# Moving the weight buffers and one activation tile in SBUF, in a decoder trunk of two layers

## The chip, the cores and the metric

One core of one Trainium2 chip runs the whole kernel. The metric is device time in microseconds, the median of the runs shown.

## The reference

Two layers act on 256 tokens of 2048 channels in float32. Layer 0 mixes tokens with an S5 state-space model and a gated projection, layer 1 with a causal depthwise convolution of 31 taps between two projections; each is followed by a SwiGLU network of 5632 hidden channels. Every sub-layer ends in a residual and a LayerNorm, with scale, shift and gate from a condition vector c. What matters here are the dense products and the loop around them, cut to its core:

```
for i in range(DEPTH):                       # DEPTH = 2
    mod = silu(c) @ ada_w[i] + ada_b[i]      # six vectors of 2048
    h = x * (1 + sc_m) + sh_m
    y = s5_mixer(h, ...)   if i == 0 else conv_mixer(h, ...)
    x = layer_norm(ALPHA * x + (1 + gt_m) * y)
    h = x * (1 + sc_f) + sh_f
    g, v = split(h @ w_gu)                   # 2048 x 11264
    y = (silu(g) * v) @ w_down               # 5632 x 2048
    x = layer_norm(ALPHA * x + (1 + gt_f) * y)
```

The result is wanted in float32 accuracy, and the kernel gets it from three products of split operands.

## The kernel before

Channels lie on partitions, tokens along the free dimension. X holds the residual stream; h (32 KB in each partition) holds the input of the current product as two parts, hh and hl, a value rounded to float32r and the rest; f2 (24 chunks of 128 hidden channels, 48 KB) holds the same of the hidden layer.

**Weights.** Every product reads its weights once from memory, in units of 512 rows by 512 columns. Unit (L834 ff.) takes a raw buffer filled by a DMA of the SP queue, ACT rounds it into whi (L835), DVE writes the rest into wlo (L836). The pool w has two buffers of each, 8 KB a partition, so that one unit is converted while the other is used.

**Matmuls.** gemm walks over the units. For each chunk of 128 input channels it computes hi times hi, wlo times hi and whi times lo. In the wide form (L891) a 128x128 block of tokens and channels of x, out of h or f, is held in TensorE and 512 columns of whi or wlo stream past it; each unit gives 24 such matmuls, each with a held block of its own. In the narrow form (L895), used where the output must come out with channels on partitions, a 128x128 block of the weights is held and 256 columns of h or f stream. A panel after each LayerNorm (L1007, Entry.panel) is like the narrow form, but streams 258 columns out of a tile raw, which is h itself or the space of f2, in rows of 258. Results of the wide form are turned back by L907. Loading the next held block overlaps the current matmul.

**Beside the matmuls.** DVE adds up the condition's projections (L703) from rawa, and computes the taps of some convolution channels (L1633); the other channels go through TensorE (L1672, four matmuls side by side, each with 32 held columns).

**Where the tiles lie.** Pools are placed one behind the other in each partition: the long-lived tiles (X, h and others), four raw buffers, further constants, the pool w, the pools s and ada of small tiles, and then f2, or the convolution's tiles (V, pad, vs, lw) in the same space. f0 and f1 are the pools of f2 for the two layers. Addresses in bytes in a partition, as the programs before and after have them:

| tile | before | after | modulo 512, before / after |
|---|---|---|---|
| h | 37824 | 37824 | 448 / 448 |
| whi, first and second | 113344, 121536 | 113344, 121600 | 192, 192 / 192, 256 |
| wlo, first and second | 129728, 137920 | 129856, 138112 | 192, 192 / 320, 384 |
| first tile of the pool s | 146112 | 146304 | 192 / 384 |
| f2 of layer 0 | 177088 | 177280 | 448 / 128 |
| f2 of layer 1 | 177088 | 177568 | 448 / 416 |

A held block of h or f starts a multiple of 512 bytes, and a moving row of whi or wlo a multiple of 2048 bytes, behind its tile's start; so the last column tells all starts modulo 512. "Distance" below is the start of the moving operand minus that of the held block loaded beside it.

Of the kernel before, what the change touches and what calls it, by code (L numbers as in the profile page):

```python
# [11 lines left out]
F32 = mybir.dt.float32  # L12
F32R = mybir.dt.float32r
# [6 lines left out]
P = 128  # L20
# [487 lines left out]
def kernel(  # L508
# [71 lines left out]
    def load_unit(src, k0, kn, segs, eng=nc.sync):  # L580

        r = raws[0].tile([P, 4, 512], F32, tag="raw", name="raw")
        if kn > 4:
            r = r.rearrange("p a b -> p (a b)").rearrange("p (k n) -> p k n", k=kn)
        raws.append(raws.pop(0))
        at = 0
        for c0, n in segs:
            eng.dma_start(r[:, :kn, at:at + n], src[k0 * P:(k0 + kn) * P, c0:c0 + n].rearrange("(k p) n -> p k n", p=P))
            at += n
        return r  # L590

    class Later:


        def __init__(self):
            self.now, self.todo = 0, []
# [17 lines left out]
    def queue_behind(instructions):  # L614

        st = ExitStack()
        for i in instructions:
            st.enter_context(tc.issue_after(i.ins))
        return st
# [206 lines left out]

    class Unit:


        def __init__(self, wp, wsrc, k0, kn, segs, behind=()):  # L830
            r = load_unit(wsrc, k0, kn, segs)
            self.hi = wp.tile([P, 4, 512], F32R, tag="whi", name="whi")
            self.lo = wp.tile([P, 4, 512], F32R, tag="wlo", name="wlo")
            with queue_behind([*behind, *held_back]):  # L834
                m1 = nc.scalar.copy(out=self.hi[:, :kn], in_=r[:, :kn])  # L835
                m2 = nc.vector.tensor_tensor(out=self.lo[:, :kn], in0=r[:, :kn], in1=self.hi[:, :kn].bitcast(F32), op=SUB)  # L836
            self.marks = [m1, m2]
            nonlocal newest
            newest = self
# [219 lines left out]
    def residual(y, gt, ch, stats=None):  # L1059

        for k in range(2):
            nc.vector.scalar_tensor_tensor(
                out=X[:, ch + k], in0=y[:, k], scalar=gt[:, ch + k:ch + k + 1], in1=X[:, ch + k], op0=MUL, op1=ADD)
        if stats is None:
            return
        i, z = ch // 2, X[:, ch:ch + 2]
        if i == 0:
            later.put(1, lambda: stats.begin(z))
            later.put(1, lambda: stats.add(0, z))
            for p in range(1, 8):  # L1070
                later.put(1 if p == 1 else 2 + p % 2, lambda p=p: stats.move(X[:, 2 * p:2 * p + 2]))
        elif i == 1 and later.todo:
            later.put(1, lambda: stats.add(1, z))
        else:
            stats.add(i, z)
# [23 lines left out]
    def add_later(ys, gt, ch, stats, sp):  # L1099

        yt = [sp.tile([P, 2, SEQ], F32, tag="sg", name="yt", bufs=2).rearrange("p a b -> p (a b)") for _ in range(2)]
        nc.scalar.copy(out=yt[0], in_=ys[0].rearrange("p a b -> p (a b)"))
        nc.vector.tensor_copy(out=yt[1], in_=ys[1].rearrange("p a b -> p (a b)"))
        for i in range(2):
            turning.put(2, lambda i=i: turned(yt, 256 * i, lambda b: residual(b, gt, ch + 2 * i, stats)))

    def gu_cols(f):
        return [(f * P, 256), (DFF + f * P, 256)]
# [205 lines left out]
    w = s5.work  # L1314
# [71 lines left out]
    mctx = ExitStack()  # L1386

    def start_dense():
        nonlocal const2, wp
        const2 = ctx.enter_context(tc.tile_pool(name="const2", bufs=1, reuse_waits="tile"))  # L1390
        wp = mctx.enter_context(tc.tile_pool(name="w", bufs=2, reuse_waits="tile"))
        ready.append(Unit(wp, s5_w_glu[0], 0, 4, [(0, 256), (D, 256)]))

    const2 = wp = ln_col = wtap = fold32 = row_of = None
# [14 lines left out]
    with tc.manual_schedule(engines={mybir.EngineType.PE}):  # L1409
# [9 lines left out]
        for ct in range(NCH - 1):  # L1419
            now, y = coming, None  # L1420
            if (ct + 1) % 4 == 1 and ct < 12:
                load_x(ct // 4 + 1)
            s5.weights_in(ct + 1)
            n = plan[ct + 1]
            ada_units(n > 0)
            with queue_behind([] if ct else [s5.made]):
                tabs[ct + 1] = s5.tables(ct + 1, [last])
            if held:
                y = s5.read_out(*held)
            u, uh, last = inputs(ct + 1)  # L1430
            ada_units(n > 1)
            coming = ct + 1, u, s5.drive(ct + 1, uh)
            if not ct:
                s5.weights_out(0, d_col[:, 0:1], last)
            s5.weights_out(ct + 1, d_col[:, ct + 1:ct + 2], last)
            ada_units(n - 2)
            if ct == NCH - 2:
                raws[:] = [rawp]
                more.close()
                s5.keep_ctx.close()  # L1440
                start_dense()
            scan(ct, now, y)
            if ct % 4 == 3 and ct < 11:
                extra = quarter_steps(ct // 4 + 2)
            with queue_behind([s5.last]):
                next(extra, None)
# [53 lines left out]
    def entry_raw(fp):  # L1500
        t = fp.tile([P, 24, 2, SEQ], F32R, tag="f2", name="raw").rearrange("p a h b -> p (a h b)")
        return t[:, 0:2 * NCH * EW]
# [5 lines left out]
    with mctx:  # L1508
# [4 lines left out]
        def enter(name, stats, i, k, raw, pairs):  # L1513

            layer, j = (i, 3) if k == 0 else (i + 1, 0)
            ada.finish(layer, j)
            ada.finish(layer, j + 1)
            g, b = ln_gb(i, k)
            hg, hb = fold(name, g, b, mod[layer][:, j + 1], mod[layer][:, j])
            e = Entry(sp, stats, raw, hg, hb, scaled(name + "xg", g, ALPHA), scaled(name + "xb", b, ALPHA))  # L1520
            for p in range(pairs):
                later.put(1 + p // 2, lambda p=p: e.split(p))
            return e
# [4 lines left out]
        for i in range(8):  # L1528
            if i == 7:
                fp = f0ctx.enter_context(tc.tile_pool(name="f0", bufs=1, reuse_waits="tile"))  # L1530
# [204 lines left out]
        for q in range(4):  # L1735
            if q == 3:
                ada.hold = True
                raw = entry_raw(fp)
                entry = enter("f1", stats, 1, 0, raw, 6)
            wide = q in (1, 2)  # L1740
            ys = gemm(cv_w_pw2[0], 0, NCH, [(512 * q, 512)], xh, wp, feed if q == 0 else None,
                      ahead=(ffn_w_gu[1], gu_cols(0)) if q == 3 else None, wide=wide)
            if wide:
                add_later(ys, mod[1][:, 2], 4 * q, stats, sp)
            for i in range(0 if wide else 2):
                residual(ys[i], mod[1][:, 2], 4 * q + 2 * i, stats)
                if q == 3:
                    entry.split(6 + i)
            if q == 0:
                cvctx.close()  # L1750
                fp = f1ctx.enter_context(tc.tile_pool(name="f1", bufs=1, reuse_waits="tile"))
        ada.hold = False
        stats = Stats("ln11", sp, True)
        ada.rate = 0.5
# [26 lines left out]
```

## Time and profile before

| | |
|---|---|
| median of 3 runs | 2292.09 us (2291.61 to 2294.86) |
| profiled execution, as timed | 2298.0 us |
| its span, first to last instruction | 2295.8 us |
| mean granted TensorE clock | 0.992 |
| busy: PE, PEld, DVE, ACT, POOL | 2223.8, 1799.3, 1691.1, 1015.6, 156.0 us |
| read from HBM | 573.72 MB, 251 GB/s over the span |

PE is TensorE's matmuls, PEld its weight loads. The duration of a matmul in the profile reaches to its modelled end and overlaps the next one; what a stream of them costs is the spacing of their starts. The chain of work is followed back from the last instruction through what released each step.

### The profile page before, as it was taken

To read this page: it belongs to the slowest core of one execution; us is meant where nothing else is said; L and a number is where in the kernel's file an instruction comes from. 1 tells how busy PE (TensorE), PEld (TensorE's weight loads), DVE (VectorE), ACT (ScalarE), POOL (GpSimd) and SP (SyncE) were. 2 spreads that over 40 slices of the span, in tenths; PEclk is the share of its full clock that TensorE was granted. 3 is DMA by queue.
4 is the path that set the end of the run, shared out by engine and by line. 5 is a ranking of instruction groups with operands and counts; after the bars stand their busy time and mean duration, and the time that the engine had idled before them with its cause. 6 is when DMAs were issued, how large, how long until landed. Compare 5 with 4: busy or idle time off the path is not lost.

```text
span 2295.8 us, 33563 instructions
## 1 busy us (share of the span) xinstructions
PE 2223.8 (97%) x13619; PEld 1799.3 (78%) x13619; DVE 1691.1 (74%) x1941; ACT 1015.6 (44%) x1253; POOL 156.0 (7%) x268
## 2 busy tenths in 40 slices
PE   6888999999999999999999998999999999999999
PEld 4555777987777887787898776898888888888888
DVE  8899888887787777787989788878755444545474
ACT  4665334644334333434446333556443333343343
POOL 5662000000000000000010110000000000000000
PEclk9999999999999999999999999999999999999999
DMA  9889799488998998999866774766875555565542
GB/s 333 288 298 301 270 329 347 161 300 310 321 320 323 325 323 308 324 323 322 307 203 195 213 214 163 276 206 203 291 234 190 188 191 189 184 193 191 185 166 92
DMA packets 380608, 579.48 MB, mean 252 GB/s; under 512 B 13875, under 2 KB 277939, under 8 KB 365987
## 3 DMA queue, kind: packets, MB, share of 16 engines
q1 hardware_dynamic: 379862, 576.82, 74.3%
q8 instruction: 107, 1.75, 0.3%
q0 software_dynamic: 352, 0.45, 0.1%
q14 instruction: 47, 0.39, 0.0%
q10 hardware_dynamic: 240, 0.08, 0.0%
HBM read 573.72 MB, written 3.57 MB: 251 GB/s over the span
## 4 chain that ended last, share of the span: by engine, by line
PE 69%; DVE 13%; DMA 9%; ACT 5%; issue 3%; SPq 0%; POOL 0%; DVEq 0%; ACTq 0%
PE acc L891 55%; PE acc L895 6%; DMA raw<-in_ffn_w_gu_dram 5%; DVE wlo L836 4%; ACT whi L835 3%; DVE adaacc L703 2%; DMA raw<-in_ffn_w_down_dram 2%; PE acc L1007 2%; PE turned L907 1%; PE conv L1672 1%; DMA raw<-in_s_w_glu_dram 1%; DVE pin L464 1%; PE y L501 1%; PE ada L632 1%; DMA raw<-in_ada_w_dram 1%
## 5 line engine op out<-in xcount | busy, mean ns | idle before, releaser
L836 DVE TENSOR_TENSOR wlo<-raw,whi 128x2048 fp32r<-128x2048 f32 x344 | 788.9, 2294 | 462.5 <-ACT whi L835 460.8
L835 ACT CAST whi<-raw 128x2048 fp32r<-128x2048 f32 x344 | 655.6, 1906 | 826.3 <-PE acc L891 407.1
L891 PE MATMUL acc<-whi,h 128*128 128x512 f32 x3648 | 889.2, 393 | 11.3 <-ACT whi L835 11.0
L891 PEld LDWEIGHTS acc<-whi,h 128*128 128x128 f32 x3648 | 677.3, 188 | 166.0 <-ACT whi L835 18.8
L891 PE MATMUL acc<-wlo,h 128*128 128x512 f32 x1824 | 461.7, 390 | 1.0 <-DVE wlo L836 0.9
L891 PEld LDWEIGHTS acc<-wlo,h 128*128 128x128 f32 x1824 | 341.6, 188 | 74.3 <-DVE wlo L836 3.7
L891 PE MATMUL acc<-whi,f 128*128 128x512 f32 x1248 | 300.9, 391 | 0.0
L703 DVE SCALAR_TENSOR_TENSOR adaacc<-rawa,c_act,adaacc 128x2048 f32<-128x2048 f32 (+1 forms) x135 | 284.5, 2107 | 0.4
L891 PEld LDWEIGHTS acc<-whi,f 128*128 128x128 f32 x1248 | 232.8, 188 | 49.5 <-ACT whi L835 1.7
L891 PE MATMUL acc<-wlo,f 128*128 128x512 f32 x624 | 156.4, 389 | 0.0
L891 PEld LDWEIGHTS acc<-wlo,f 128*128 128x128 f32 x624 | 117.1, 188 | 24.3
L1602 POOL TENSOR_TENSOR lw<-fold,wtap 128x1024 f32<-128x1024 f32 x12 | 26.3, 2195 | 1064.1 <-PE acc L895 874.8
L632 PE MATMUL ada<-raw,c_rep 128*32 128x512 f32 (+1 forms) x576 | 71.3, 591 | 5.7 <-DMA raw<-in_ada_w_dram 3.7
L1240 ACT ACTIVATE fsg<-acc 128x256 f32<-128x256 f32 x84 | 31.6, 379 | 96.2 <-PE acc L891 96.2
L895 PE MATMUL acc<-h,whi 128*128 128x256 f32 x512 | 67.3, 286 | 4.2 <-DVE h L1705 2.2
L895 PEld LDWEIGHTS acc<-h,whi 128*128 128x128 f32 x512 | 63.6, 192 | 9.9 <-ACT h L911 4.3
L1184 POOL CAST lnmh<-lno 128x2 fp32r<-128x2 f32 x1 | 0.2, 181 | 885.3 <-DVE lno L68 885.3
L1241 DVE TENSOR_TENSOR fsg<-acc,fsg 128x256 f32<-128x256 f32 x84 | 35.0, 418 | 16.0 <-ACT fsg L1240 16.0
L464 DVE TENSOR_TENSOR_SCAN pin<-rho,pin 128x256 f32<-128x256 f32 x64 | 44.2, 691 | 1.5
L1672 PE MATMUL conv<-vs,lw 128*32 128x256 f32 x720 | 42.2, 380 | 0.1
L895 PE MATMUL acc<-f,whi 128*128 128x256 f32 x320 | 40.7, 284 | 0.0
L895 PEld LDWEIGHTS acc<-f,whi 128*128 128x128 f32 x320 | 39.3, 192 | 0.2
(349 smaller groups left out, 1852.8 us busy)
## 6 DMA issues: line engine op xcount, KB each, us to landing
raw<-in_ffn_w_gu_dram SPq DMA_DIRECT2D x352, 512.0 KB, 4.7
rawa<-in_ada_w_dram SPq DMA_DIRECT2D x128, 1024.0 KB, 5.6
raw<-in_ffn_w_down_dram SPq DMA_DIRECT2D x88, 1024.0 KB, 5.1
raw<-in_ada_w_dram SPq DMA_DIRECT2D x64, 1024.0 KB, 7.6
raw<-in_s_w_glu_dram SPq DMA_DIRECT2D x64, 512.0 KB, 6.1
raw<-in_cv_w_pw_dram SPq DMA_DIRECT2D x64, 512.0 KB, 5.9
raw<-in_cv_w_pw_dram SPq DMA_DIRECT2D x16, 1024.0 KB, 5.9
vs<-scr SPq DMA_DIRECT2D x40, 142.0 KB, 5.5
```

What stands on the lines that cost most here:

```text
L464: v.tensor_tensor_scan(out=z, data0=rh[:, a].rearrange("p r h c -> p (r h c)"), data1=z, initial=0.0, op0=MUL, op1=ADD)
L632: nc.tensor.matmul(acc[32 * (k % 4):32 * (k % 4) + 32, :], c_rep[:, kk, :], r[:, k, :], start=kk < 4, stop=kk >= NCH - 4)
L703: nc.vector.scalar_tensor_tensor(out=acc, in0=r[:, i], scalar=c_act[:, kk:kk + 1], in1=acc, op0=MUL, op1=ADD)
L835: m1 = nc.scalar.copy(out=self.hi[:, :kn], in_=r[:, :kn])
L836: m2 = nc.vector.tensor_tensor(out=self.lo[:, :kn], in0=r[:, :kn], in1=self.hi[:, :kn].bitcast(F32), op=SUB)
L891: nc.tensor.matmul(acc[bank].rearrange("p a b -> p (a b)"), x[:, bank * HALF:(bank + 1) * HALF], wt[:, k], start=first, stop=end)
L895: nc.tensor.matmul(acc[bank][:, i], wt[:, k, m * P:(m + 1) * P], x, start=first and i == 0, stop=end and i == 1)
L1007: nc.tensor.matmul(acc[m][:, 0:EW], wt[:, k, m * P:(m + 1) * P], xx[:, 4 * u + k], start=u == 0 and n == 0, stop=u == 3 and n == len(order ...
L1240: nc.scalar.activation(out=t[:, i], in_=gv[:, 0], func=AF.Sigmoid)
L1241: nc.vector.tensor_tensor(out=t[:, i], in0=gv[:, 0], in1=t[:, i], op=MUL)
L1602: nc.gpsimd.tensor_tensor(out=lw, in0=fold32.unsqueeze(1).unsqueeze(1).broadcast_to([P, 4, CONV_G, 32]), in1=bc(wtap[:, :, 4 * (ch + k):4 ...
L1672: nc.tensor.matmul(acc[32 * q:32 * q + 32, :], lw[:, q, g, :], vs[:, q, 4 * g:4 * g + SEQ], start=g == 0, stop=g == n - 1)
```

## The change

Whi and wlo get a tag for each buffer, and their four tiles are claimed in a fixed order with a gap of 16 floats (64 bytes) ahead of each but the first. A unit's number, even or odd, chooses its pair, as the rotation of two buffers did before. Whatever lies behind moves on by 192 bytes. In layer 1 a tile of 72 floats (288 bytes) is claimed ahead of f2, which thus moves by 480 bytes. The gaps are never written or read. Each engine has the same instructions in the same order, with the same waits (1352 rows of PE, 1638 of DVE, 921 of ACT, 218 of POOL and 321 of SP when like instructions are merged, in both programs); only operand addresses differ.

```
     class Unit:
+        count = 0
         def __init__(self, wp, wsrc, k0, kn, segs, behind=()):
             r = load_unit(wsrc, k0, kn, segs)
-            self.hi = wp.tile([P, 4, 512], F32R, tag="whi", name="whi")
-            self.lo = wp.tile([P, 4, 512], F32R, tag="wlo", name="wlo")
+            n = Unit.count % 2
+            Unit.count += 1
+            self.hi = wp.tile([P, 4, 512], F32R, tag=f"whi{n}", name="whi")
+            self.lo = wp.tile([P, 4, 512], F32R, tag=f"wlo{n}", name="wlo")
...
     def start_dense():
...
-        wp = mctx.enter_context(tc.tile_pool(name="w", bufs=2, reuse_waits="tile"))
+        wp = mctx.enter_context(tc.tile_pool(name="w", bufs=1, reuse_waits="tile"))
+        for i, tag in enumerate(("whi0", "whi1", "wlo0", "wlo1")):
+            if i:
+                wp.tile([P, 16], F32, name=f"gap{i}")
+            wp.tile([P, 4, 512], F32R, tag=tag, name="place")
...
             if q == 0:
                 cvctx.close()
                 fp = f1ctx.enter_context(tc.tile_pool(name="f1", bufs=1, reuse_waits="tile"))
+                fp.tile([P, 72], F32, name="gap4")
```

## The prediction

> **What bounds the kernel now.** I read the page's busy shares and its chain of work first. Per line: share of the span; the last line gives the chain by line.
>
> ```profile
> span 2295.8 us, 33563 instructions
> PE 2223.8 (97%) x13619; PEld 1799.3 (78%) x13619; DVE 1691.1 (74%) x1941; ACT 1015.6 (44%) x1253; POOL 156.0 (7%) x268
> PE 69%; DVE 13%; DMA 9%; ACT 5%; issue 3%; SPq 0%; POOL 0%; DVEq 0%; ACTq 0%
> PE acc L891 55%; PE acc L895 6%; DMA raw<-in_ffn_w_gu_dram 5%; DVE wlo L836 4%; ACT whi L835 3%; DVE adaacc L703 2%; DMA raw<-in_ffn_w_down_dram 2%; PE acc L1007 2%; PE turned L907 1%; PE conv L1672 1%; DMA raw<-in_s_w_glu_dram 1%; DVE pin L464 1%; PE y L501 1%; PE ada L632 1%; DMA raw<-in_ada_w_dram 1%
> ```
>
> TensorE is busy 97% of the span, and the wide matmuls of L891 carry 55% of the chain. So only a change in the spacing of matmuls can move the end by much. The page's groups say how many there are (behind the bar: busy us, mean ns of one, and after the next bar the idle time before it):
>
> ```profile
> L891 PE MATMUL acc<-whi,h 128*128 128x512 f32 x3648 | 889.2, 393 | 11.3 <-ACT whi L835 11.0
> L891 PE MATMUL acc<-wlo,h 128*128 128x512 f32 x1824 | 461.7, 390 | 1.0 <-DVE wlo L836 0.9
> L891 PE MATMUL acc<-whi,f 128*128 128x512 f32 x1248 | 300.9, 391 | 0.0
> L891 PE MATMUL acc<-wlo,f 128*128 128x512 f32 x624 | 156.4, 389 | 0.0
> ```
>
> That is 3648 + 1824 + 1248 + 624 = 7344 wide matmuls. The 390 ns is from a matmul's start to its modelled end and overlaps the next; the spacing has to be read from unbroken pieces of the chain (start us, length us, what):
>
> ```profile
> 1809.90 32.70 PE acc L891 x144
> 1877.04 32.66 PE acc L891 x144
> 1698.74 21.79 PE acc L891 x96
> 402.20 17.27 PE acc L895 x144
> 434.20 10.80 PE acc L1007 x90
> 1198.32 10.81 PE acc L1007 x90
> 1547.25 10.79 PE acc L1007 x90
> ```
>
> 512 moving columns take 32.70 / 144 = 227.1 and 32.66 / 144 = 226.8 ns, 226.9 on average (held operand f), and 21.79 / 96 = 227.0 ns (held operand h). 256 columns on L895 take 17.27 / 144 = 119.9 ns. The difference, 107.0 ns for 256 columns, is 0.418 ns a column; so 226.9 - 214.0 = 12.9 ns, say 13, stands between two matmuls beside the columns. This 13 ns is the only thing in the trace that a layout could take away or make larger, 7344 times.
>
> **The change part by part.** It adds no instruction and takes none away: the rows on each engine and the waits in them are the same in both programs, and only addresses differ. So each term is a count times a change of duration.
>
> *Wide matmuls.* While whi or wlo streams, the next 128x128 block of h or f is loaded. Counted in bytes modulo 512, the moving operand now starts 256 behind the held one in every wide matmul, whichever buffers are used. After the change the four buffers stand at 256, 320, 384 and 448 against h, at 64, 128, 192 and 256 against layer 0's f2, and at 288, 352, 416 and 480 against layer 1's. The first buffer of whi against h keeps its distance (half of 3648), and so does the second of wlo against layer 0's f2 (a quarter of 624); that leaves 7344 - 1824 - 156 = 5364, say 5400, with a new one. What a distance is worth has no row of its own for wide matmuls, since the trace has only one. Two neighbours have many.
>
> The first is the panel of L1007, whose moving tiles lie 1032 bytes apart, so that the distance takes 32 values in steps of 8 bytes. Duration is min/median/max:
>
> ```profile
> L1007 PEld LDWEIGHTS acc<-raw,wlo x128: 187/190/193, 421.1 to 1555.7; 128*128 128x128 f32 x128
> L1007 PE MATMUL acc<-raw,wlo x128: 277/283/292, 421.2 to 1555.8; 128*128 128x258 f32 x128
> L895 PEld LDWEIGHTS acc<-f,wlo x160: 192/192/193, 1156.1 to 2279.1; 128*128 128x128 f32 x160
> L895 PE MATMUL acc<-f,wlo x160: 282/283/284, 1156.2 to 2279.2; 128*128 128x256 f32 x160
> ```
>
> There single matmuls scatter from 277 to 292 ns and loads from 187 to 193, where L895, at one distance, shows 282 to 284 and 192 to 193. Something at the 6 to 9 ns level does move. Yet the pieces above give 10.80 / 90 = 120.0 ns for L1007 against 119.9 for L895: the scatter is given back by the next matmul, and the mean does not know the distance.
>
> The second neighbour is the convolution (L1672), the only other place where streaming of moving columns sets the pace. Its moving and held operands stand at 16 different distances modulo 512, in multiples of 16 bytes:
>
> ```profile
> 1254.69 3.66 PE L1672 MATMUL conv<-vs,lw 128*32 128x256 f32 x64
> 1262.81 3.66 PE L1672 MATMUL conv<-vs,lw 128*32 128x256 f32 x64
> 1304.84 3.66 PE L1672 MATMUL conv<-vs,lw 128*32 128x256 f32 x64
> 1370.01 3.66 PE L1672 MATMUL conv<-vs,lw 128*32 128x256 f32 x64
> ```
>
> 64 matmuls take 3.66 us whichever channel chunk and buffers they use. Its loads are 32 columns and not 128, which is why it does not settle the case alone. Bounds for the wide term: a gain of all 13 ns, 5400 x 13 = 70 us; a loss of 9 ns, L1007's 292 - 283, 5400 x 9 = 49 us. I take 0, since both neighbours with many distances keep their mean.
>
> The Trainium skill ("SBUF — State Buffer", Who interferes with whom) says outright that TensorE waits for nobody at SBUF and has one read port for the moving operand and another for weight loads. By that rule the change is worth exactly 0; L1007's scatter of 277 to 292 ns shows that its picture is not the whole of it, but not that the mean moves.
>
> *Narrow matmuls.* L895 has 1248 and L1007 has 576. The two lines' spacings are 119.9 and 120.0 at one and at many distances, so between them 0.1 ns x 1824 = 0.2 us. Ends: minus 4 ns, should L895's 192 ns loads become the 188 ns of other places and set the pace, -5 us; plus 1 ns (193 - 192), +2 us. I take 0: L1007 has loads of 190 ns in the median and is no quicker.
>
> *Casts and vector work on moved tiles.* ACT writes whi and DVE writes wlo, 344 times each, and all of the pool of small tiles moves by 192 bytes.
>
> ```profile
> L835 ACT CAST whi<-raw x344: 1887/1906/1927, 217.1 to 2265.2; 128x2048 fp32r<-128x2048 f32 x172
> L836 DVE TENSOR_TENSOR wlo<-raw,whi x344: 2272/2292/3715, 219.7 to 2267.2; 128x2048 fp32r<-128x2048 f32 x172
> L1633 DVE SCALAR_TENSOR_TENSOR vacc<-vpad,taps,vacc x45: 468/474/2193, 1239.8 to 1370.5; 128x256 f32<-128x256 f32 x45
> L1633 DVE SCALAR_TENSOR_TENSOR vacc<-pad,taps,vacc x26: 469/475/480, 1382.5 to 1415.2; 128x256 f32<-128x256 f32 x26
> ```
>
> The taps of L1633 read at every 4-byte offset; but for a few that wait (2193), they stay within some 12 ns, with medians of 474 and 475: 0.2%. Lines 835 and 836 are 3% and 4% of the chain, 161 us of 2295.8; 0.2% of it is +-0.3 us. The rest of the casts lies beside matmuls, so a quicker or slower one changes idle time alone. I take 0. If a cast did grow, PE would wait for whi next: it already does for 11 us on L891.
>
> *Transfers.* The raw buffers that receive the weights do not move. The convolution's scratch tiles move by a multiple of 64 bytes, and no DMA queue is issued in another order: 0. The place-holding tiles and gaps are never written: 0.
>
> Sum: 0. Against the profiled execution that is 2295.8 us of span, 2298.0 us as timed. That execution is 5.9 us above the median of 2292.09 us, so the forecast for the median stays at 2292.
>
> **The rivals.** A measurement of this kernel tells 0.2%, 4.6 us, from no change; over 5400 matmuls that is 0.85 ns each. From there either rival decides.
>
> *Faster: the 13 ns is a collision of the two reads.* The held block and the moving row always meet at 256 modulo 512; were that the cause of the 13 ns, new distances would end it. All of it gives 2292 - 70 = 2222, a quarter 2274. For: it is one fixed distance, the gap is equal in every long piece, and L1007 has single steps shorter than its mean. Against: L1007's many distances leave 120.0, and in the convolution all are alike. In a sentence of its own: the Trainium skill ("TensorE: Matmul & The Clock Gate", Wait — 56ns, not 53.3ns?) gives the columns at 2.4 GHz plus about 2.5 ns for matmuls back to back, 215.8 ns for 512 columns. By that rule 11 ns of the 226.9 are not TensorE's own, and if the layout caused them the estimate is 5400 x 11 = 59 us, 2233. No row here shows a 512-column matmul at that spacing, which is why I hold this the likelier rival and not the forecast.
>
> *Slower: the fixed distance is a good one.* At 256 modulo 512 all reads keep a steady step (282 to 284 ns on L895), and other distances bring L1007's late ones, 292 instead of 283 ns. In L1007 a late one is followed by an early one, because there the weight load sets the pace; a wide matmul is paced by its stream, so lateness might add up. At a third of the 9 ns, 5400 x 3 = 16 us, 2308; at all of it 2341.
>
> *The change does not do what it says.* All gaps but layer 1's extra 288 bytes are multiples of 64. If what matters repeats within 64 bytes, only layer 1's 624 + 312 of f sees anything new (936 x 9 = 8 us at the very most, 936 x 13 = 12 us the other way). It mostly gives 2292 again and belongs to the forecast.
>
> **How the numbers follow.** Forecast, no measurable change, 0.67 (the distance doesn't matter to the mean, 0.5, or repeats within 64 bytes, 0.17). Collision ended wholly or in part, 0.19. New collisions, 0.14. These are the chances of same, faster and slower. Predicted is the likeliest, 2292. For 8 in 10 the range goes into both rivals: down to 2272 (20 us, 4 ns of the 13 on 5400 matmuls), up to 2306 (14 us, under 3 ns); what lies beyond I put at 0.12 below and 0.08 above. Alone, the forecast would have 2287.5 to 2296.7.
>
> **What would show it.** Right: pieces of L891 in the chain still at 226.9 ns a matmul, for h and for f; L895 at 119.9 or with L1007's scatter around the same mean; casts at 1906 and 2292 ns; busy PE within 1% of 2223.8 us. Wrong on the wide term: pieces of 144 clearly off 32.68 us, and differently for the two layers' f, since their distances differ. If whi's and wlo's groups part from each other, buffers are good or bad one by one. Wrong on casts: other medians on L835 or L836, and more than 11 us of waiting for whi before L891.

## The result, and the profile after

The changed kernel takes 2308.74 us, the median of 5 runs (2306.1 to 2317.1); beside it the kernel before takes 2292.99 us, the median of 5 (2291.61 to 2294.86). The ratio is 1.0072, 95% interval 1.0051 to 1.0093: slower by 0.7%, some 16 us. The forecast was 2292, with a range up to 2306. The profiled execution of the changed kernel took 2306.29 us. In what follows, two experiments (f1_alone and all_64) have no profile that can be read, because their profiled executions were disturbed and took 7.3 and 4.5 ms; these executions are left out of their times below, and their kernels were run once more as f1_alone_b and all_64_b.

The page of the changed kernel: span, busy times, and the chain by engine and by line. Line 891 of before is 894 now, 895 is 898, 1007 is 1010, and the casts of 835 and 836 are 838 and 839.

```profile
span 2303.7 us, 33563 instructions
PE 2242.4 (97%) x13619; PEld 1796.4 (78%) x13619; DVE 1692.2 (73%) x1941; ACT 1016.5 (44%) x1253; POOL 156.5 (7%) x268
PE 82%; DVE 10%; ACT 4%; DMA 3%; issue 2%; POOL 0%; SPq 0%; DVEq 0%; ACTq 0%
```

No instruction came or went, and PE's busy time grew from 2223.8 to 2242.4 us. PE's share of the chain grew from 69% to 82%, and DMA's shrank from 9% to 3%. About half of this is a difference between executions, since all_64_b below, which has before's distances, shows 75% and 5%. The groups of the changed kernel, with mean ns behind the busy time:

```profile
L894 PE MATMUL acc<-whi,h 128*128 128x512 f32 x3648 | 896.1, 394 | 4.8 <-ACT whi L838 4.4
L894 PE MATMUL acc<-wlo,h 128*128 128x512 f32 x1824 | 471.2, 395 | 0.4 <-DVE wlo L839 0.2
L894 PE MATMUL acc<-whi,f 128*128 128x512 f32 x1248 | 307.5, 396 | 0.0
L894 PE MATMUL acc<-wlo,f 128*128 128x512 f32 x624 | 160.0, 395 | 0.0
```

The four groups were 889.2, 461.7, 300.9 and 156.4 us: all four grew, wlo with h by 2.1% and whi with h, half of which kept its distance, by 0.8%. The sum of the gains is 26.6 us. The pieces of the chain say it directly (start us, length us):

```profile
766.87 33.28 PE acc L894 x144
...
1843.37 33.63 PE acc L894 x144
...
2082.20 22.14 PE acc L894 x96
```

A matmul with 512 moving columns takes 33.28 / 144 = 231.1 ns with layer 0's f, 33.63 / 144 = 233.5 with layer 1's f, and 22.14 / 96 = 230.6 with h. All three were 227 before. The narrow matmuls went the other way, and their neighbour L1010 stayed:

```profile
396.70 16.63 PE acc L898 x144
428.08 10.80 PE acc L1010 x90
```

16.63 / 144 = 115.5 ns instead of 119.9; L1010 is at 120.0 as before. Worked out from the starts of neighbouring matmuls in the two traces (intervals with a wait in them left out), wide matmuls went from 227.2 to 231.0 ns on average (7088 intervals), narrow ones of L898 from 119.9 to 117.3 (1209), L1010 from 119.9 to 119.8. Times their counts that is 7344 x 3.8 = +28 us and 1248 x 2.6 = -3 us. The end moved by only 16, and the stages show why. Each row is a window (start and end us, its length), then busy us and instruction counts of PE, PEld, DVE, ACT, POOL, the granted clock, the DMA share and GB/s. First two windows of the changed kernel, then the stretches of before that hold the same work:

```profile
480.00:900.00 420.00, 418.51 (x1867) 337.30 (x1866) 320.86 (x216) 165.40 (x131) 0.00 (x0) 1.00 0.91 321
1553.00:2276.00 723.00, 723.00 (x3293) 591.05 (x3292) 400.80 (x335) 300.46 (x256) 0.00 (x0) 1.00 0.58 194
```

```profile
480.00:900.00 420.00, 412.53 (x1859) 335.13 (x1859) 320.22 (x215) 164.23 (x129) 0.00 (x0) 1.00 0.90 319
1558.00:2268.00 710.00, 710.00 (x3291) 590.88 (x3290) 400.62 (x335) 300.44 (x256) 0.00 (x0) 1.00 0.60 197
```

From 1553 us on, in layer 1's feed-forward, PE is busy throughout: 3293 matmuls take 723 us where 3291 took 710, so all of the slower spacing is paid, 13 us, nearly 4 ns each. From 480 to 900 us as many matmuls run in 420 us as before, 1867 against 1859. There the DMA engines are 0.90 to 0.91 busy and deliver some 320 GB/s in both kernels, and PE's idle time is what shrinks: 420 - 412.53 = 7.5 us before, 1.5 after. The cast's waits for weights tell the same (total us, count, mean us), the changed kernel first, then before:

```profile
ACT whi L838 <- DMA raw<-in_ffn_w_gu_dram: 136.4, 46, 5.8
```

```profile
ACT whi L835 <- DMA raw<-in_ffn_w_gu_dram: 173.4, 57, 6.3
```

So a part of the slower matmuls is lost in a wait that was there anyway. How large a part is less sure: all_64_b runs 1883 matmuls in these 420 us, with 3.2 us of idle time, and its cast waits 156.9 us in 55 waits, so some of what these lines show is a difference between executions. The granted clock is 1.00 in all four windows, so it is not the clock.

### The profile page after: what moved, and what is told of

Its sections match the earlier page's. It is cut to its first block, busy times and chain, and to the rows that moved or that the text cites. A ratio compares the mean times of both kernels' runs of the same rounds, so it can differ in the third digit from the quotient of the medians.

```text
span 2303.7 us, 33563 instructions
## 1 busy us (share of the span) xinstructions
PE 2242.4 (97%) x13619; PEld 1796.4 (78%) x13619; DVE 1692.2 (73%) x1941; ACT 1016.5 (44%) x1253; POOL 156.5 (7%) x268
## 4 chain that ended last, share of the span: by engine, by line
PE 82%; DVE 10%; ACT 4%; DMA 3%; issue 2%; POOL 0%; SPq 0%; DVEq 0%; ACTq 0%
PE acc L894 67%; PE acc L898 5%; DVE wlo L839 2%; PE acc L1010 2%; PE turned L910 2%; ACT whi L838 2%; PE conv L1679 1%; DMA raw<-in_ffn_w_gu_dram 1%; DVE pin L464 1%; PE y L501 1%; DVE adaacc L703 1%; DMA raw<-in_s_w_glu_dram 1%; DMA raw<-in_ada_w_dram 1%; PE ada L632 1%; DVE x L452 0%
## 5 line engine op out<-in xcount | busy, mean ns | idle before, releaser
L894 PE MATMUL acc<-wlo,h 128*128 128x512 f32 x1824 | 471.2, 395 | 0.4 <-DVE wlo L839 0.2
L894 PE MATMUL acc<-whi,f 128*128 128x512 f32 x1248 | 307.5, 396 | 0.0
L898 PE MATMUL acc<-h,whi 128*128 128x256 f32 x512 | 66.1, 284 | 3.7 <-ACT h L914 2.4
L898 PEld LDWEIGHTS acc<-h,whi 128*128 128x128 f32 x512 | 62.4, 191 | 9.2 <-ACT h L914 4.4
L898 PE MATMUL acc<-f,whi 128*128 128x256 f32 x320 | 40.1, 282 | 0.0
L898 PEld LDWEIGHTS acc<-f,whi 128*128 128x128 f32 x320 | 38.8, 189 | 0.2
```

The source lines that it names most:

```text
L894: nc.tensor.matmul(acc[bank].rearrange("p a b -> p (a b)"), x[:, bank * HALF:(bank + 1) * HALF], wt[:, k], start=first, stop=end)
L898: nc.tensor.matmul(acc[bank][:, i], wt[:, k, m * P:(m + 1) * P], x, start=first and i == 0, stop=end and i == 1)
```

## The experiments

Three theories stood after the result. D: the spacing depends on the distance between the start of the moving operand and that of the held block loaded beside it, and each distance has its price. A: the address of the operand itself counts (a buffer that starts at a multiple of 512 bytes is quick). M: the mixture counts (buffers at several distances in turn). The distances below are moving start minus held start in bytes modulo 512, in the order h, layer 0's f, layer 1's f; before has 256, 256, 256 in every buffer. Spacings "from the starts" are means over all neighbouring matmuls of a kind with no wait between them.

**One part of the change alone.** gaps_alone is the changed kernel without its line `fp.tile([P, 72], F32, name="gap4")`, so layer 1's f stands as layer 0's. f1_alone is the kernel before with layer 1's f moved alone:

```diff
                 fp = f1ctx.enter_context(tc.tile_pool(name="f1", bufs=1, reuse_waits="tile"))
+                fp.tile([P, 120], F32, name="gapf1")
```

> The gaps between the weight buffers as in the change, but layer 1's f2 without its extra 288 bytes (distances modulo 512: h 256/320/384/448, f of both layers 64/128/192/256). Theory D, the spacing of wide matmuls follows from the distances that occur: layer 1's f goes to what layer 0's f had in the changed kernel, 230 to 232 ns instead of 233 to 235, which takes 936 x 2.3 ns = 2 us off; total 2303 to 2308 us. Theory F, moving layer 1's f2 was the main cost: total within 0.2% of 2293. Rival N, the change's loss is an effect of the run and not of the layout: 2293 as well, and L891 back at 227 ns a matmul.

> Only layer 1's f2 is moved, by 480 bytes; all four weight buffers stay alike, so that f of layer 1 has one new distance (288 modulo 512) and everything else the old one. Theory D (each distance has its own price): L891 with layer 1's f at about 233.3 ns, as at 288 in the changed kernel, 936 x 6.5 ns = 6 us more, 2299 us; h and layer 0's f stay at 226.9. Theory M (mixing several distances costs, a single one does not): 226.9 ns at 288 too, 2293 us.

> The kernel with layer 1's f2 alone moved once more, for its trace. Theory D: L891 with layer 1's f at 233.3 ns, with h and layer 0's f at 226.9.

gaps_alone took 2309.2 us (2306.71 to 2311.64) against 2290.86 of before, ratio 1.0076 (1.0061 to 1.0091). f1_alone took 2297.8, ratio 1.0028 (1.0011 to 1.0046), some 6 us. The one run of f1_alone_b took 2304.08, 6 us above the profiled execution of before (2298.0). The chain of gaps_alone, then of f1_alone_b:

```profile
1846.39 33.37 PE acc L894 x144
...
2084.46 22.14 PE acc L894 x96
```

```profile
1844.69 33.60 PE acc L891 x144
...
2036.88 21.79 PE acc L891 x96
```

In gaps_alone layer 1's f has the spacing of layer 0's, 33.37 / 144 = 231.7. In f1_alone_b it stands at 288 and takes 33.60 / 144 = 233.3 ns, while h, untouched, keeps 227.0. So the matmuls whose distance was changed slow down, and those alone. With 936 matmuls x 6.4 ns = 6.0 us, f1_alone's loss agrees with D. Of the whole loss the gaps between the weight buffers carry all that can be measured: gaps_alone is not below the changed kernel, though theory D gave it some 2 us less, which is smaller than these intervals.

**Moving both operands.** all_64 puts 64 bytes ahead of h, so that it and all behind it move together and every distance stays 256:

```diff
+    const.tile([P, 16], F32, name="gaph")
```

> A gap of 64 bytes ahead of h, so that h, the weight buffers, f2 and all small tiles behind them move by 64 bytes together: every distance between held and moving operands stays at 256 modulo 512, only addresses change. Theory D or M (distances matter): L891 at 226.9 ns, L895 at 119.9, total within 0.2% of 2293 us. Rival A (the address of an operand matters, for instance where it starts within 512 bytes): spacing changes by several ns on all of L891, total more than 5 us away from 2293.

> The kernel with everything from h on moved by 64 bytes once more, for its trace. Theory D: L891 at 226.9 and L895 at 119.9 ns throughout.

Its time was 2294.7 us, ratio 1.0013 (1.0002 to 1.0023); the single run of all_64_b gave 2288.52. The interval leaves out no change by a hair, in a size that another run of the kernel does not repeat, and the chain of all_64_b shows none:

```profile
1868.16 32.66 PE acc L892 x144
...
2046.46 21.82 PE acc L892 x96
```

226.8 and 227.3 ns, and the narrow matmuls keep 119.9 from the starts. Theory A falls: with both operands 64 bytes on, the spacing stays, so what counts is what lies between them. Since all_64_b has the distances of before, it also serves to compare stages. Worked out from the starts, the changed kernel's 2000th matmul of lines 894, 898 and 1010 comes 1.6 us earlier than in all_64_b, its 6000th 4.3 us later, the 8000th 12.8 and the 9000th 16.9: most of the loss arises after 1550 us, where PE is busy throughout and no wait is left to take it up.

**One distance for all buffers.** w64, w128, w192, w256 and w32 leave the weight buffers where they stand to each other (8192 bytes apart) and move all four together by that many bytes, with f of each layer moved as well; so in each kernel h, layer 0's f and layer 1's f have one distance each, without a mixture. The edit of w64; the others have other sizes, and w32 moves f2 within its tile by 16 and 8 bytes:

```diff
         wp = mctx.enter_context(tc.tile_pool(name="w", bufs=2, reuse_waits="tile"))
+        wp.tile([P, 16], F32, name="gapw", bufs=1)
...
+                fp.tile([P, 16], F32, name="gapf0")
...
+                fp.tile([P, 32], F32, name="gapf1")
```

> One gap of 64 bytes ahead of the pool of weight buffers and none between them, and f2 moved by a further 64 bytes in layer 0 and 128 in layer 1: one distance each, 320 for h, 192 for layer 0's f, 128 for layer 1's f (modulo 512). Theory D: each of the three has a spacing of its own on L891, near the changed kernel's means at these distances (320: 229.9; 192: 232.3; 128: 232.6), total 2293 + 5472 x 3 ns + 1872 x 5.5 ns = 2320 us or less where waits absorb it. Theory M: all three at 226.9 ns and 2293 us.

> One gap of 128 bytes ahead of the weight buffers, f2 moved by 192 further in layer 0 and 256 in layer 1: single distances of 384 for h, 64 for layer 0's f, 0 for layer 1's f. Theory D (a price for each distance): L891 at 232.5 ns with h and 230.5 with layer 0's f, as in the mixed kernels at 384 and 64; 0 is new. Theory P (only multiples of 256 are cheap): 0 gives 226.9 ns as 256 does. Theory B (256 is dear and a better distance exists): 0 gives less than 226.

> Gap of 256 ahead of the weight buffers: 0 for h; f2 moved so that layer 0's f has 32 and layer 1's f has 96. Theory P: h at 226.9 ns and the total within 0.5% of 2291 us; 32 and 96 at 230 ns or more. Theory B: h under 226 ns, the total up to 50 us less. Theory D alone leaves h open between 224 and 236 ns, the values seen so far for single matmuls.

> Gap of 192: 448 for h, 480 for layer 0's f, 416 for layer 1's f. Theory D: L891 at 232.3, 232.5 and 234.7 ns, as in the changed kernel at these distances, whether they are mixed or alone; total 2291 + 5472 x 5.3 ns + 1872 x 6.7 ns = 2333 us, less what waits absorb (they took about a third to a half so far): 2310 to 2325 us.

> Gap of 32 ahead of the weight buffers: 288 for h; f2 begins 16 bytes into its space in layer 0 and 8 in layer 1, so that its distances are 240 and 248. Theory D: h at 233.3 ns as layer 1's f at 288 in the changed kernel, total 2291 + 5472 x 6.4 ns = 2326 us less what waits absorb. If distances count in steps below 32 bytes, 240 and 248 leave 226.9 ns too; if they count in 32 bytes or more, both stay within 1 ns of it.

w64 took 2306.32 us (2304.37 to 2307.67), ratio 1.0062 (1.0047 to 1.0077), with no mixture of distances: theory M falls as a main cause. The other four are single runs, beside one run of before of 2285.08: w256 2303.95, w128 2312.84, w32 2323.02, w192 2330.93. The totals of w256 and w192 lie above those expected (at most 2302.5 and 2325); their spacings came within about 1 ns of what was expected, so in w192 the allowance for waits was too large, as far as a single run tells. Each chain, a piece with layer 1's f and one with h:

w64 (128 and 320):

```profile
1843.75 33.46 PE acc L891 x144
...
2058.79 21.99 PE acc L891 x96
```

w128 (0 and 384):

```profile
1852.66 32.69 PE acc L891 x144
...
2044.51 22.32 PE acc L891 x96
```

w256 (96 and 0):

```profile
1844.45 33.59 PE acc L891 x144
...
2081.15 21.78 PE acc L891 x96
```

w192 (416 and 448):

```profile
1862.88 33.73 PE acc L891 x144
...
2080.87 22.40 PE acc L891 x96
```

w32 (248 and 288):

```profile
1857.86 33.26 PE acc L891 x144
...
2051.65 22.39 PE acc L891 x96
```

A distance of 0 gives 32.69 / 144 = 227.0 ns with f and 21.78 / 96 = 226.9 with h, as 256 did. All others are slower, and by amounts that repeat from kernel to kernel and from operand to operand. From the starts, the wide matmul's price by distance modulo 256, with the places where it was seen:

| distance | ns | seen as |
|---|---|---|
| 0 | 226.6 to 227.7 | 256 in before and all_64_b, 0 in w256 (h) and w128 (f) |
| 32 | 233.2 to 233.4 | 288 in w32 (h) and f1_alone_b (f), 32 in w256 (f) |
| 64 | 228.7 to 229.2 | 320 in w64 (h), 64 in w128 (f) |
| 96 | 232.9 to 233.7 | 96 in w256 (f) |
| 128 | 232.3 to 232.7 | 384 in w128 (h), 128 in w64 (f) |
| 160 | 234.2 to 234.3 | 416 in w192 (f) |
| 192 | 233.2 to 233.4 | 448 in w192 (h), 192 in w64 (f) |
| 224 | 233.2 to 233.4 | 480 in w192 (f) |
| 240 | 229.7 to 231.8 | 240 in w32 (f) |
| 248 | 230.7 to 230.8 | 248 in w32 (f) |

Wherever both halves of the 512 were seen, the price is the same: it repeats every 256 bytes, not every 64, and 8 bytes off a good distance already cost 4 ns. No distance tried is quicker than 0. Before happened to stand at the best of them in every wide matmul.

With these prices the changed kernel can be read buffer by buffer. From the starts, layer 1's f takes 233.3 ns at 288 and 234.7 at 416, within half a ns of the table. Others differ from it by a ns or more either way: layer 0's f takes 230.5 at 64, h 232.3 at 448. And whi's first buffer with h takes 229.2 at 256 where before has 227.0, and wlo's second with layer 0's f 230.7 at 256 where before has 226.7. So a good distance in the midst of bad ones loses 2 to 4 ns: a mixture does cost something, though it isn't the main cause. The order within a unit shows where it does: of the 16 matmuls of whi's first buffer with h, the first ten average 225 to 235 ns and the last six 227.0, in gaps_alone as well. It looks as if what is lost follows the change from another distance and dies out; why, these runs do not show.

**The narrow matmuls.** They had become quicker in the changed kernel, so two kernels try to take that gain alone. narrow_64 keeps the wide matmuls at 0 modulo 256, with the weight buffers 8448 bytes apart, and shifts the weights of narrow ones by 64 bytes within their buffers, f being moved by 192 bytes; narrow_panel adds the same for the panel of L1007 (rows of 1280 instead of 1032 bytes):

```diff
-            self.hi = wp.tile([P, 4, 512], F32R, tag="whi", name="whi")
-            self.lo = wp.tile([P, 4, 512], F32R, tag="wlo", name="wlo")
+            n = Unit.count % 2
+            Unit.count += 1
+            self.hi, self.lo = (
+                wp.tile([P, 2048 + 16], F32R, tag=f"{t}{n}", name=t)[:, off:off + 2048].rearrange("p (k n) -> p k n", n=512)
+                for t in ("whi", "wlo"))
...
+                w = Unit(wp, wsrc, k0 + u0, kn, segs, feed.marks if feed and u == 1 else (), 0 if wide else 16)
...
-        return t[:, 0:2 * NCH * EW]
+        return t[:, 48:48 + 2 * NCH * 320].rearrange("p (r n) -> p r n", n=320)[:, :, 0:EW].rearrange("p (k a) n -> p k a n", a=2)
```

(The last two lines are narrow_panel's alone.)

> Wide matmuls keep a distance of 0 modulo 256 everywhere (the buffers stand 8448 bytes apart), and the units that narrow matmuls use begin 64 bytes into their buffers, so that L895's 1248 matmuls have 192 modulo 256. Theory D, with the prices measured so far: L891 at 226.9, L895 at 113.5 to 114.4 ns instead of 119.9, 1248 x 5.8 ns = 7 us less than before, 0.3%. Rival W (narrow stretches are paced by weights and not by matmuls): L895 at 114 ns, but the total within 0.1% of before.

> As the run before, and the two panels that stream out of f2's space get rows 1280 bytes apart instead of 1032, each at 192 modulo 256 from the held blocks. Theory D: 384 of L1007's matmuls at 114 to 115 ns instead of 120, 2 us more of gain, 9 us and 0.4% in all. Rival: a panel of 258 columns keeps 120 ns, since its scatter comes from the 258 columns and not from the distances.

narrow_64 took 2286.66 us (2283.73 to 2297.04) against 2291.46, ratio 0.9989 (0.9974 to 1.0004), which is not told from no change; narrow_panel 2286.7 (2282.86 to 2289.45), ratio 0.9981 (0.9973 to 0.9990), 0.2%, some 4 us, below before. In the chain of narrow_panel, L902 is the narrow line, L1015 the panel, L898 the wide one:

```profile
397.03 16.35 PE acc L902 x144
428.18 10.89 PE acc L1015 x90
...
1865.08 32.69 PE acc L898 x144
```

The narrow piece fell from 17.27 to 16.35 us, 113.5 ns a matmul, and the wide one kept 227.0. The panel did not gain: 10.89 / 90 = 121.0 ns, and its single matmuls still last 280 to 289 ns (min/median/max ns):

```profile
L1015 PE MATMUL acc<-raw,wlo x128: 280/283/289, 415.1 to 1544.0; 128*128 128x258 f32 x128
```

So what narrow_panel gains on before is narrow_64's part, and of the about 9 us expected half came. The panel's rows of 258 columns, or something else in it, keep it at 120 whatever its distance; which of these was not tried. Nor did every narrow matmul reach 113.5: from the starts, layer 1's f took 116.3 to 117.8 ns at the same distance at which layer 0's took 113.3 to 114.8. A distance can have two steady spacings here: in the changed kernel wlo's second buffer with h stands at 64 and takes 113.3 to 114.1, where w192 has 117.5 at 64. What selects one stays open. The other kernels show the narrow spacing at one distance for all of h: 119.8 to 120.0 at 0 modulo 256 (before, w256), 114.3 to 114.5 at 192 (w64), 118.7 at 128 (w128), 117.5 at 64 (w192), 118.3 at 224 (w32).

## Why the prediction was wrong

The step that failed is the wide term: "I take 0, since both neighbours with many distances keep their mean." It measured 3.8 ns on 7344 matmuls, 28 us. Neither neighbour could tell what a distance does to a wide matmul.

The panel's rows lie 1032 bytes apart, so they pass through the whole period of 256 bytes in steps of 8 in every layout, and shifting all of them cannot change their mean: it is 119.7 to 120.0 from the starts in before and in the kernels with moved buffers, w192 among them, whose wide matmuls are the slowest. Its single rows do say something, and something else than was needed. In before they average 118 to 122 ns, none near the 113 of a narrow matmul at 192, and narrow_panel's, all at 192, keep 120.4 to 120.8. So the panel is indifferent to the distance where the other two kinds are not.

The convolution was no test in the changed kernel, since its moving and held tiles lie in one pool and move together. A piece of 64, which averages over its own distances, takes what it took before, by the same view of operations in order of time:

```profile
1250.17 3.66 PE L1679 MATMUL conv<-vs,lw 128*32 128x256 f32 x64
```

The prediction noted that its loads are 32 columns and not 128, "which is why it does not settle the case alone", and then let it settle the case together with a second witness of another shape. The trace of before could not give the price itself, since its wide matmuls have one distance only.

The rival "slower: the fixed distance is a good one" had the right mechanism: at other distances the wide matmuls come late and the lateness adds up, so that the mean spacing grows. That it met the measured 16 us (5400 x 3 ns, 2308) is luck. The matmuls whose distance changed lost 4.4 ns each, 5364 x 4.4 = 23 us, those that kept theirs lost another 5 us beside them, the narrow ones gave 3 back, and 9 us of the rest did not reach the end. Its reason, that the weight load sets the pace in the panel, is not shown: the narrow matmuls have loads of the same size and do change with the distance. The rival was given 0.14 after the neighbours had been read as speaking against any effect, and that reading also put the range's upper end at 2306.

The signs that the prediction named were the right ones: pieces of 144 went from 32.68 to 33.28 us with layer 0's f and 33.63 with layer 1's, and whi's and wlo's groups parted. One was too coarse: PE's busy time stayed within 1% of 2223.8 us (2242.4, 0.8% more) though the forecast failed.

The rule of the Trainium skill ("SBUF — State Buffer", Who interferes with whom), that TensorE waits for nobody at SBUF, gave exactly 0. The runs disagree: 226.6 to 234.3 ns for the same wide matmul by the distance between what it streams and what is loaded beside it.

The rival "faster: the 13 ns is a collision" fell in the form in which it was put: no distance of the ten in the table beats 0, so before's 256 is no collision that one of these distances ends. Whether the 13 ns beside the columns at distance 0 are TensorE's own stays open.

"If what matters repeats within 64 bytes, only layer 1's f sees anything new" was wrong too: gaps of 64 bytes carry the loss, and the period is 256.

The narrow term's zero was off by 3 us, in the direction of its lower end of -5: loads of 192 ns did become 188 where the distance moved. The reason for 0 had been that L1007 has loads of 190 ns in the median and is no quicker; L1007 is no measure for this line either. The loads (first row) and the matmuls in the changed kernel, which were 192/192/193 and 282/283/284:

```profile
L898 PEld LDWEIGHTS acc<-f,wlo x160: 187/188/193, 1151.2 to 2286.9; 128*128 128x128 f32 x160
L898 PE MATMUL acc<-f,wlo x160: 277/280/287, 1151.4 to 2287.1; 128*128 128x256 f32 x160
```

The casts were right at 0. Their medians are the 1906 and 2292 ns of before:

```profile
L838 ACT CAST whi<-raw x344: 1887/1906/1913, 215.3 to 2273.3; 128x2048 fp32r<-128x2048 f32 x172
L839 DVE TENSOR_TENSOR wlo<-raw,whi x344: 2274/2292/3721, 217.9 to 2275.2; 128x2048 fp32r<-128x2048 f32 x172
```

Transfers were right at 0 as well: 0.91 of the DMA engines and 321 GB/s between 480 and 900 us, against 0.90 and 319.

What the sum lacked altogether is the cover: 28 - 3 = 25 us more on PE became 16 at the end (12 to 21 by the interval). The prediction counted 5400 matmuls at full price in its bounds; in the stages that wait for weights, a slower matmul first uses up the wait. How much that takes is not settled. In w64 the same sum gives 7344 x 2.9 - 1248 x 3.9 = 16 us, and 14 were paid. In w192 it gives 7344 x 6.2 - 1248 x 2.0 = 43, and its single run lies 46 us above the run of before beside it, 40 above the median of other runs (2291).

## What to carry to other kernels

Layout in SBUF is a variable of speed for matmuls back to back: keep the start of a 512-column moving operand and that of the held block at a multiple of 256 bytes from each other; any other distance tried cost 2 to 7 ns of 227, and the narrow matmuls wanted another one (192 modulo 256, 113 to 118 instead of 120 ns). So a new tile of a few bytes ahead of a weight buffer can move a kernel's time by a per cent with no instruction changed (0.7% here, 1.7 to 2% in the single run of w192), and a comparison of two versions should look at the spacing of matmuls first. To price a term from a neighbour, take one of the same shape, and one that holds each value of what changes apart: a mean over all distances cannot show what one distance costs.

## What was not expected of the hardware

The spacing of one and the same matmul depends on the distance of its two operands in SBUF with a period of 256 bytes, and 8 bytes matter (230.8 ns at 248, 227 at 256). Moving both operands by 64 bytes together changes nothing (226.8 and 227.3 ns). Best distances differ by shape: 512 moving columns are quickest at 0 (226.9 ns), 256 moving columns quickest at 192 (113.3 to 114.8, in one place 116.3 to 117.8) and slow at 0 (119.9), where the weight load takes 192 instead of 188 ns. A mixture of distances slows wide matmuls that are good in themselves (229.2 and 230.7 ns at 256), and one distance can show two steady spacings (113.3 and 117.5 ns at 64). Why the period is 256 and what collides was not settled by these runs.
